# MLP of a hybrid decoder layer: first weight casts ahead of the first relus, the residual's scale and shift in four parts, other PSUM banks and another block order in the last group

## The chip, the cores and the metric

The kernel runs on one core of one Trainium2 chip. The metric is the device time of one execution in microseconds (us), as the median of several runs. PE is the matrix engine (TensorE), DVE the vector engine, ACT the scalar engine, POOL GpSimd, and SP the engine whose queue issues most transfers. Each engine runs its own instructions in the order in which the program emits them, and waits at an instruction until the semaphores of what it needs are set.

## The reference, cut to what matters

One decoder layer on 512 tokens and 16 meta tokens, width 1024, float32: attention and a recurrent mixer, then an output projection with a layer norm, then the MLP. The change touches the MLP alone:

```python
    h = layer_norm(ALPHA * h + merged @ w_out[l], ln1_g[l], ln1_b[l])
    ff = jnp.square(jax.nn.relu(h @ w_ff1[l])) @ w_ff2[l]      # 1024 -> 4096 -> 1024
    h = layer_norm(ALPHA * h + ff, ln2_g[l], ln2_b[l])
return h[:, N_META:]
```

## The kernel before, in words

Each float32 operand of a product is split into a rounded part (`hi`, by a cast on ACT) and its rest (`lo`, by a subtraction on DVE), and each product is the sum of three: hi by hi, lo by hi and hi by lo. So every weight tile costs a load on the SP queue, casts on ACT, subtractions on DVE, and then the matmuls.

**Up products.** The 4096 hidden columns are 32 tiles of 128. Tile f takes 24 matmuls of 128x512 (8 pieces of the width, three products each), then a relu on ACT (line 1604) and a square on DVE (line 1605), and lands in `ff`, a buffer for one group of 8 tiles, of which there are two. The first three tiles (`SPLITF`, lines 1530 to 1544) belong to the front part of the kernel, whose instructions stand in a fixed list (`ORDER`); they are computed in two halves of 256 tokens, in segments of six matmuls of 256 columns. The last segments in the list, by tile and segment of the second half, are (f0,1), (f0,2), (f1,2), (f1,3), (f2,2), (f0,3), (f2,3). Their weights lie in the three `whi` and three `wlo` slots of the pool `wst`, each slot cut into two halves of 512 columns: the first `whi` slot holds the second half of tile 1 and the first half of tile 2, the first `wlo` slot the first half of tile 1 and the second half of tile 2. A tile's first half is read by segments 0 and 1, its second by 2 and 3. The other tiles' weights go through the same slots in turn, beginning with the first.

**Down products.** The hidden columns are taken in four groups of 8 tiles (`NG`). In the first three groups the product of `ff` (two blocks of tokens t by two blocks of columns x) with w_ff2 (two blocks x by two halves of the output d) is made of seven block products in place of eight (`down`, lines 1670 to 1717), with sums and differences of blocks: the sums of weights are added on DVE (line 1685), the differences of hidden blocks too (line 1701), the right blocks are split by `split_right` (two tile pairs, from the rings `b` and `w`), the left block by `split_left` (ring `a`, two pairs). Each product is 24 matmuls into two PSUM banks, and is added into the residual `res` (four row blocks b, two halves d) by two DVE additions (line 1715). The pairs of banks are called u (up products), R, P and T. The last group (`last_group`, lines 1721 to 1765) makes the eight plain block products, and then ends each of the four row blocks: two additions (line 1745), statistics for each half (line 1566), their merging, a power on POOL, four scalings (lines 1572 and 1573) and two stores (`finish`).

**The residual.** Before the first down product is added, `res` is multiplied by ALPHA and ln1's gain (line 1771, eight instructions) and then gets ALPHA times ln1's offset added (eight more). `first_rows` loads both vectors, spread over all partitions, 512 KB each.

**The order.** All of this is a list of units: five up units (tiles 3 to 7), then up and down units in turn, then the last group. One loop (line 1799) emits them: at step i the loads of unit i+4, the preparation (casts, subtractions) of unit i+2, the matmuls of unit i, and its `post` (relu and square, additions, scalings). Before this loop, the relus and squares of the first three tiles are emitted. So ACT and DVE see three relus and squares, then the preparations of units 0 and 1, and so on; the eight scalings stand behind unit 2, the eight shifts behind unit 3, and the preparation of the first down unit (unit 6) comes behind those.

Of the kernel before, what the change touches and what calls it, by code (L numbers as in the profile page):

```python
# [20 lines left out]
P = 128  # L21
D = 1024
# [3 lines left out]
T = SEQ + NMETA  # L26
# [58 lines left out]
SPLITF = 3  # L85
# [296 lines left out]
def hybrid_layer_kernel(ctx: ExitStack, tc: tile.TileContext, I: dict, out: bass.AP):  # L382
# [1179 lines left out]
    st2 = [rp.tile([P, 2, 6], F32, name=f"gst{b}") for b in range(4)]  # L1562

    def finish(b, g2, b2):
        for n in range(2):
            dve.bn_stats(st2[b][:, n, :], res[b][n])  # L1566
# [64 lines left out]
    def block_of(g, t, x):  # L1631
        return ff[g].rearrange("p (i x) (t c) -> p i x t c", x=2, t=2)[:, :, x, t]
# [4 lines left out]
            nc.sync.dma_start(raws[g, x, d].rearrange("p i c -> p (i c)"), I["w_ff2"][(2 * g + x) * 2 + d])  # L1637
        return f

    def split_left(src):  # L1640
        hi, lo = pair_of("a")
        v = lambda t: t.rearrange("p (i c) -> p i c", c=256)
        act.copy(v(hi), src)
        dve.tensor_tensor(v(lo), src, v(hi).bitcast(F32), op=ALU.subtract)
        return hi, lo
# [11 lines left out]
    def products(left, right, acc, bs, first, last, again=False):  # L1657
        (ahi, alo) = left
        for b in bs:
            for i in range(NP):  # L1660
                bhi, blo = right[i // 2]
                as_ = slice(i * 256 + b * P, i * 256 + (b + 1) * P)
                ws = slice((i % 2) * 512, (i % 2 + 1) * 512)
                for q, (l, r) in enumerate(((ahi, bhi), (ahi, blo), (alo, bhi))):
                    pe.matmul(acc[b], l[:, as_], r[:, ws], start=first and i == 0 and q == 0,  # L1665
                              stop=last and i == NP - 1 and q == 2, skip_group_check=True)
# [3 lines left out]
    def down(g, n):  # L1670
        left, chain, updates = (
            ((1, 0),                 "R", (2, 0, ALU.add)),
            (((1, 1), (1, 0)), "T", (2, 0, ALU.add)),
            (((0, 1), (1, 0)), "R", (2, 1, ALU.subtract)),
            ((0, 1),                 "P", (0, 1, ALU.add)),
            (((1, 0), (0, 0)), "R", (0, 1, ALU.subtract)),
            (((1, 1), (0, 1)), "P", (2, 1, ALU.add)),
            (((0, 0), (0, 1)), "R", (0, 0, ALU.add)),
        )[n]
        first = n in (0, 1, 3)  # L1680
        loads = [[load_raw(g, 0, 0), load_raw(g, 1, 0)], [], [load_raw(g, 0, 1)], [load_raw(g, 1, 1)], [], [], [load_raw(g, 0, 0)]][n]
        s = {}

        def plus(a, b):
            dve.tensor_tensor(a, a, b, op=ALU.add)  # L1685
            return a

        def prep():
            x0, y0, x1, y1 = (raws.get((g, x, d)) for d in range(2) for x in range(2))
            if n == 0:  # L1690
                chains["sum"] = plus(x0, y0)
            elif n == 2:
                plus(chains["sum"], x1)
            elif n == 3:
                plus(chains["sum"], y1)
            elif n == 6:
                plus(x0, x1)
            right = (chains["sum"], y0, chains["sum"], chains["sum"], x1, y1, x0)[n]
            if isinstance(left[0], tuple):
                src = mp.tile([P, NP, 256], F32, name="dif", tag="dif", bufs=2)  # L1700
                dve.tensor_tensor(src, block_of(g, *left[0]), block_of(g, *left[1]), op=ALU.subtract)
            else:
                src = block_of(g, *left)
            s["r"] = split_right(right)
            s["l"] = split_left(src)

        def run():
            if first:
                chains[chain] = [psum(chain, i, f"dn{chain}") for i in range(2)]
            products(s["l"], s["r"], chains[chain], range(2), first, True)  # L1710

        def post():
            b, d, op = updates
            for i in range(2):
                dve.tensor_tensor(res[b + i][d], res[b + i][d], chains[chain][i], op=op)

        return Unit(loads, prep, run, post)
# [1 line left out]
    rows_ = {}  # L1719

    def last_group(g):
        accs, sets, lefts = {}, {}, {}

        def unit(t, x, ds, bs, loads=(), lefts_=(), rights=(), post=lambda: None):
            def prep():
                for x_, d in rights:
                    sets[x_, d] = split_right(raws[g, x_, d])
                for k in lefts_:
                    lefts[k] = split_left(block_of(g, *k))

            def run():
                for d in ds:
                    if (t, d) not in accs:
                        accs[t, d] = [psum(*[("R", i), ("T", i), ("P", i), ("u", i)][2 * t + d], "last") for i in range(2)]
                for b in bs:
                    for d in ds:
                        products(lefts[t, x], sets[x, d], accs[t, d], [b], x == 0, x == 1)

            return Unit(loads, prep, run, post)

        def done(t, b):
            def f():
                for d in range(2):
                    r = res[2 * t + b][d]
                    dve.tensor_tensor(r, r, accs[t, d][b], op=ALU.add)  # L1745
                finish(2 * t + b, rows_["g"], rows_["b"])
            return f

        def vectors():
            t = mp.tile([P, 2, D], F32, name="rows2", tag="ff", bufs=2)  # L1750
            rows_["g"], rows_["b"] = t[:, 0], t[:, 1]
            row_of(t[:, 0], "ln2_g")
            row_of(t[:, 1], "ln2_b")
# [12 lines left out]

    def scaled(name, k):
        def f():
            for b in range(4):
                for n in range(2):  # L1770
                    dve.scalar_tensor_tensor(  # L1771
                        res[b][n], *((res[b][n], ALPHA, rows_["1"][:, k, n * 512 : (n + 1) * 512]) if k == 0 else
                                     (rows_["1"][:, k, n * 512 : (n + 1) * 512], ALPHA, res[b][n])),
                        op0=ALU.mult, op1=(ALU.mult, ALU.add)[k])
        return f

    def first_rows():
        t = rows_["1"] = mp.tile([P, 2, D], F32, name="rows1", tag="braw", bufs=4)
# [1 line left out]
        row_of(t[:, 1], "ln1_b")  # L1780

    units = [up(f) for f in range(SPLITF, NF)]
    units[1].loads.append(first_rows)
    for i, k in ((2, 0), (3, 1)):
        was = units[i].post
        units[i].post = lambda was=was, k=k: (was(), scaled(None, k)())
    for g in range(NG - 1):
        f = (g + 1) * NF
        for n in range(7):
# [3 lines left out]
                units.append(up(f))  # L1793
                f += 1
            units.append(down(g, n))
    units += last_group(NG - 1)
    for f in range(SPLITF):
        up_evict(f, ups[f].t)
    for i in range(-LEAD[0], len(units)):
        if 0 <= i + LEAD[0] < len(units):  # L1800
            for f in units[i + LEAD[0]].loads:
                f()
        if 0 <= i + LEAD[1] < len(units):
            units[i + LEAD[1]].prep()
        if i >= 0:
            units[i].run()
            units[i].post()
# [52 lines left out]
```

## Time and profile before

| what | us |
|---|---|
| median of 3 runs | 918.55 (917.95 to 919.69) |
| the profiled execution, its own time | 918.13 |
| its span, first to last instruction | 916.4 |
| PE busy | 885.1 (97% of the span) |
| DVE, ACT, POOL busy | 668.6, 471.1, 245.8 |
| mean granted PE clock | 0.988 |

In the rows of a timeline the columns are: start (us from the span's start), us, engine, line of the kernel, operation, the tile written and the tiles read, the shape, how many; in brackets the idle time of the engine before and what ended it. Consecutive instructions of one kind are merged into one row. In the rows of the windows the busy time of PE, of its weight loads (PEld), of DVE, ACT and POOL follow one another, then the granted clock (1.00 is full speed), the share of the DMA engines and the GB/s. A line is that of a helper where the work goes through one: L466 to L468 are the three products of `three`, L1665 is the matmul of the down products.

### The profile page before, as it was taken

To read this page: it belongs to the slowest core of one execution; us is meant where nothing else is said; L and a number is where in the kernel's file an instruction comes from. 1 tells how busy PE (TensorE), PEld (TensorE's weight loads), DVE (VectorE), ACT (ScalarE), POOL (GpSimd) and SP (SyncE) were. 2 spreads that over 40 slices of the span, in tenths; PEclk is the share of its full clock that TensorE was granted. 3 is DMA by queue.
4 is the path that set the end of the run, shared out by engine and by line. 5 is a ranking of instruction groups with operands and counts; after the bars stand their busy time and mean duration, and the time that the engine had idled before them with its cause. 6 is when DMAs were issued, how large, how long until landed. Compare 5 with 4: busy or idle time off the path is not lost. (4 is left out here: it accounts for less than half of the span.)

```text
span 916.4 us, 16744 instructions
## 1 busy us (share of the span) xinstructions
PE 885.1 (97%) x6424; PEld 761.2 (83%) x6424; DVE 668.6 (73%) x1152; ACT 471.1 (51%) x1030; POOL 245.8 (27%) x652
## 2 busy tenths in 40 slices
PE   7999999999999999999999999989999999999895
PEld 6999989888998888978878778778888888888784
DVE  7873977869677697487586788488778777877647
ACT  7845568376583674565726548333433344443410
POOL 4137173381643804606538111000000000000001
PEclk9999999999999999999989999999999999999998
DMA  7453333424242242223245522432342343232302
GB/s 267 126 132 99 88 92 89 125 67 128 71 112 68 86 143 72 60 71 113 71 131 152 142 94 82 134 153 92 115 138 93 115 143 133 92 119 91 134 1 92
DMA packets 69496, 99.02 MB, mean 108 GB/s; under 512 B 39863, under 2 KB 47289, under 8 KB 66985
## 3 DMA queue, kind: packets, MB, share of 16 engines
q1 hardware_dynamic: 68576, 96.79, 34.2%
q8 instruction: 50, 0.82, 0.4%
q10 hardware_dynamic: 840, 1.17, 0.4%
q14 instruction: 30, 0.24, 0.1%
HBM read 90.78 MB, written 8.21 MB: 108 GB/s over the span
## 5 line engine op out<-in xcount | busy, mean ns | idle before, releaser
L466 PE MATMUL g<-hhi,whi 128*128 128x512 f32 (+3 forms) x640 | 212.9, 333 | 0.5 <-DVE GR L1057 0.5
L467 PE MATMUL g<-hlo,whi 128*128 128x512 f32 (+3 forms) x640 | 204.0, 319 | 1.7 <-DVE hlo L829 1.7
L468 PE MATMUL g<-hhi,wlo 128*128 128x512 f32 (+3 forms) x640 | 203.6, 318 | 0.1
L466 PEld LDWEIGHTS g<-hhi,whi 128*128 128x128 f32 x640 | 121.0, 189 | 12.9 <-issue 1.9
L467 PEld LDWEIGHTS g<-hlo,whi 128*128 128x128 f32 x640 | 121.1, 189 | 9.6 <-DVE hlo L829 2.1
L468 PEld LDWEIGHTS g<-hhi,wlo 128*128 128x128 f32 x640 | 121.0, 189 | 8.7 <-DVE wlo L625 0.4
L625 DVE TENSOR_TENSOR wlo<-wraw,whi 128x512 fp32r<-128x512 f32 x126 | 88.5, 709 | 30.4 <-ACT whi L623 29.7
L1134 POOL TENSOR_TENSOR ftmp<-Xf,Nf 108x84 f32<-108x84 f32 (+23 forms) x248 | 86.8, 350 | 75.4 <-DMA Nf<-Nd 45.2
L623 ACT CAST whi<-wraw 128x512 fp32r<-128x512 f32 x126 | 76.9, 618 | 55.6 <-PE g L467 23.9
L458 POOL TENSOR_TENSOR rsf<-rsf,mhalf 128x1 f32<-128x1 f32 x4 | 3.9, 987 | 341.9 <-DVE rsf L457 341.9
L1138 POOL TENSOR_TENSOR Xf<-Xf,ftmp 108x84 f32<-108x84 f32 (+23 forms) x248 | 90.0, 363 | 19.0
L466 PE MATMUL up<-h1hi,whi 128*128 128x512 f32 x232 | 91.0, 392 | 1.9 <-ACT whi L1618 1.9
L468 PE MATMUL up<-h1hi,wlo 128*128 128x512 f32 x232 | 90.9, 392 | 0.2 <-DVE wlo L1619 0.2
L467 PE MATMUL up<-h1lo,whi 128*128 128x512 f32 x232 | 90.8, 391 | 0.0
L1605 DVE TENSOR_TENSOR ff<-ff 128x512 f32<-128x512 f32 x32 | 21.9, 691 | 55.5 <-ACT ff L1604 55.5
L1604 ACT ACTIVATE ff<-up 128x512 f32<-128x512 f32 x29 | 17.3, 596 | 87.2 <-PE up L468 87.2
L1652 ACT CAST bhi<-braw 128x1024 fp32r<-128x1024 f32 x25 | 26.2, 1049 | 61.1 <-DVE braw L1685 53.1
L1240 ACT ACTIVATE Z<-g,PC 64x64 f32<-64x64 f32 x64 | 19.8, 310 | 65.2 <-DVE Z L1237 40.0
L466 PEld LDWEIGHTS up<-h1hi,whi 128*128 128x128 f32 x232 | 43.8, 189 | 11.0 <-ACT whi L1618 2.1
L468 PEld LDWEIGHTS up<-h1hi,wlo 128*128 128x128 f32 x232 | 43.8, 189 | 10.1 <-DVE wlo L1619 0.9
L467 PEld LDWEIGHTS up<-h1lo,whi 128*128 128x128 f32 x232 | 43.9, 189 | 9.1
L1618 ACT CAST whi<-wraw 128x1024 fp32r<-128x1024 f32 x29 | 30.3, 1048 | 23.2 <-PE dnR L1665 12.0
(406 smaller groups left out, 2044.3 us busy)
## 6 DMA issues: line engine op xcount, KB each, us to landing
wraw<-in_w_in_dram SPq DMA_DIRECT2D x52, 512.0 KB
braw<-in_w_ff_dram SPq DMA_DIRECT2D x19, 1024.0 KB
wraw<-in_w_ff_dram SPq DMA_DIRECT2D x32, 512.0 KB
wraw<-in_w_out_dram SPq DMA_DIRECT2D x14, 256.0 KB
Nf<-Nd SPq DMA_DIRECT2D x24, 144.0 KB
res<-in_x_dram SPq DMA_DIRECT2D x4, 512.0 KB
G<-in_consts_dram SPq DMA_DIRECT2D x16, 128.0 KB
XB<-xtd SPq DMA_DIRECT2D x16, 128.0 KB
```

Source lines behind the costliest of these rows:

```text
L466: pe.matmul(ps, whi, xhi, start=first, stop=False)
L467: pe.matmul(ps, whi, xlo, start=False, stop=False)
L468: pe.matmul(ps, wlo, xhi, start=False, stop=last)
L623: AC(512, lambda hi=hi, qs=qs: act.copy(hi.t, raw.t[:, qs]), plain=True, r=[raw], w=[hi], new=[hi])
L625: f = lambda hi=hi, lo=lo, qs=qs, e=e: e.tensor_tensor(lo.t, raw.t[:, qs], hi.t.bitcast(F32), op=ALU.subtract)
L1134: sub(nj * nt, lambda s=s, nj=nj, nt=nt, tv=tv: pool.tensor_tensor(tv(), Xf.t[:, 0:nj, s : s + 1].to_broadcast([NB, nj, nt]), Nf.t[:, s : ...
L1138: sub(nj * nt, lambda s=s, nj=nj, tv=tv: pool.tensor_tensor(Xf.t[:, 0:nj, s + 1 :], Xf.t[:, 0:nj, s + 1 :], tv(), op=ALU.add), port=1, r=[ ...
L1240: op("ACT", 335, lambda: act.activation(Z.t[H2[1], c, 1, :], src(1), AF.Copy, scale=PC.t[H2[1], last : last + 1]), r=[ps, PC], w=[(Z, ("s" ...
L1604: act.activation(t, ps, AF.Relu)
L1605: dve.tensor_tensor(t, t, t, op=ALU.mult)
L1618: act.copy(hi, s["raw"])
L1652: act.copy(hi, src)
```

## The change

- `finish` no longer takes the statistics of the two halves. `done` takes each half's statistics right behind the addition that ends this half.
- `split_left` may be told which tiles to write. In the last group the left block (0,1) goes into two tiles of the ring `dif`, the block (1,1) into one tile of the ring `ff`, and the others into the ring `a` as before.
- In the seven-product groups, the second product (n = 1, banks T) is no longer added into `res` after each group. It stays in its PSUM banks over the groups, and the last group goes on adding its own block (t = 1, d = 0) to it.
- The last group runs over d = 0 first: four units with one block product each, (t,x) = (0,0), (1,0), (0,1), (1,1); then d = 1: four units, one for each row block, with both of its block products. The banks are P for (t = 0, d = 0), T for (1,0), u for (0,1) and R for (1,1). The additions and statistics of d = 0 come behind the third and the fourth unit, those of d = 1 and `finish` behind the last four. Each of the first four units loads one weight block, and ln2's vectors go into a slot of the weight blocks' ring `braw`, not of `ff`.
- The scale and shift of the residual is cut in four parts, one for each pair of row blocks t and half n: two scales, then two shifts. They come behind units 1, 2, 3 and 4, in the order (t,n) = (1,0), (1,1), (0,1), (0,0). The loads of ln1's vectors move from unit 1's loads to unit 3's.
- The relus and squares of the first three tiles are emitted inside the loop: that of tile 0 behind the preparation of unit 0, those of tiles 1 and 2 behind the preparation of unit 1.

```diff
     def finish(b, g2, b2):
-        for n in range(2):
-            dve.bn_stats(st2[b][:, n, :], res[b][n])
         mv = rp.tile([P, 2], F32, name=f"gmv{b}")
...
-    def split_left(src):
-        hi, lo = pair_of("a")
+    def split_left(src, room=None):
+        hi, lo = room or pair_of("a")
...
-        first = n in (0, 1, 3)
+        first = n in (0, 3)
...
         def run():
-            if first:
+            if first or chain not in chains:
                 chains[chain] = [psum(chain, i, f"dn{chain}") for i in range(2)]
-            products(s["l"], s["r"], chains[chain], range(2), first, True)
+            products(s["l"], s["r"], chains[chain], range(2), first or n == 1 and g == 0, n != 1)
 
         def post():
+            if n == 1:
+                return
...
     def last_group(g):
-        accs, sets, lefts = {}, {}, {}
-
-        def unit(t, x, ds, bs, loads=(), lefts_=(), rights=(), post=lambda: None):
+        sets, lefts = {}, {}
+        accs = {(1, 0): chains["T"]}
+
+        def room(t, x):
+            if (t, x) == (0, 1):
+                return tuple(mp.tile([P, D], F32R, name="a" + q, tag="dif", bufs=2) for q in ("hi", "lo"))
+            if (t, x) == (1, 1):
+                t = mp.tile([P, 2, D], F32R, name="aw", tag="ff", bufs=2)
+                return t[:, 0], t[:, 1]
+            return pair_of("a")
+
+        def unit(parts, loads=(), lefts_=(), rights=(), post=lambda: None):
...
             def run():
-                for d in ds:
+                for t, x, d, bs in parts:
                     if (t, d) not in accs:
-                        accs[t, d] = [psum(*[("R", i), ("T", i), ("P", i), ("u", i)][2 * t + d], "last") for i in range(2)]
+                        accs[t, d] = [psum({(0, 0): "P", (0, 1): "u", (1, 1): "R"}[t, d], i, "last") for i in range(2)]
+                    products(lefts[t, x], sets[x, d], accs[t, d], bs, x == 0 and (t, d) != (1, 0), x == 1)
+
+            return Unit(loads, prep, run, post)
+
+        def done(t, d, bs):
+            def f():
                 for b in bs:
-                    for d in ds:
-                        products(lefts[t, x], sets[x, d], accs[t, d], [b], x == 0, x == 1)
...
-                finish(2 * t + b, rows_["g"], rows_["b"])
+                    dve.bn_stats(st2[2 * t + b][:, d, :], r)
+                    if d == 1:
+                        finish(2 * t + b, rows_["g"], rows_["b"])
             return f
...
-            unit(0, 0, (0,), both, [load_raw(g, 0, 0), load_raw(g, 0, 1)], [(0, 0)], [(0, 0)]),
-            unit(1, 0, (0,), both, [load_raw(g, 1, 0), load_raw(g, 1, 1)], [(1, 0)]),
-            unit(1, 0, (1,), both, [vectors], (), [(0, 1)]),
-            unit(0, 0, (1,), both, (), (), [(1, 1)]),
-            unit(0, 1, both, (0,), (), [(0, 1)], [(1, 0)], done(0, 0)),
-            unit(0, 1, both, (1,), (), [], (), done(0, 1)),
-            unit(1, 1, both, (0,), (), [(1, 1)], (), done(1, 0)),
-            unit(1, 1, both, (1,), (), (), (), done(1, 1)),
+            unit([(0, 0, 0, both)], [load_raw(g, 0, 0)], [(0, 0)], [(0, 0)]),
+            unit([(1, 0, 0, both)], [load_raw(g, 1, 0)], [(1, 0)]),
+            unit([(0, 1, 0, both)], [load_raw(g, 0, 1)], [(0, 1)], [(1, 0)], done(0, 0, both)),
+            unit([(1, 1, 0, both)], [load_raw(g, 1, 1)], [(1, 1)], [(0, 1)], done(1, 0, both)),
+        ] + [
+            unit([(t, 0, 1, (b,)), (t, 1, 1, (b,))], [vectors] if t + b == 0 else (), (), [(1, 1)] if t + b == 0 else (), done(t, 1, (b,)))
+            for t in range(2) for b in range(2)
         ]
...
+    def scaled(t, n):
+        for k in range(2):
+            v = rows_["1"][:, k, n * 512 : (n + 1) * 512]
+            for b in (2 * t, 2 * t + 1):
+                r = res[b][n]
+                if k == 0:
+                    dve.scalar_tensor_tensor(r, r, ALPHA, v, op0=ALU.mult, op1=ALU.mult)
+                else:
+                    dve.scalar_tensor_tensor(r, v, ALPHA, r, op0=ALU.mult, op1=ALU.add)
...
-    units[1].loads.append(first_rows)
-    for i, k in ((2, 0), (3, 1)):
+    units[3].loads.append(first_rows)
+    for i, at in ((1, (1, 0)), (2, (1, 1)), (3, (0, 1)), (4, (0, 0))):
...
-    units += last_group(NG - 1)
-    for f in range(SPLITF):
-        up_evict(f, ups[f].t)
-    for i in range(-LEAD[0], len(units)):
...
         if 0 <= i + LEAD[1] < len(units):
             units[i + LEAD[1]].prep()
+        if i < 0 and i + LEAD[1] >= 0:
+            for f in ((0,), (1, 2))[i + LEAD[1]]:
+                up_evict(f, ups[f].t)
         if i >= 0:
             units[i].run()
             units[i].post()
```

More of the change, by code (lines that the diff above doesn't have):

```diff
@@ L1728, in prep @@
                 for k in lefts_:
-                    lefts[k] = split_left(block_of(g, *k))
+                    lefts[k] = split_left(block_of(g, *k), room(*k))
             def run():
-                for d in ds:
+                for t, x, d, bs in parts:
                     if (t, d) not in accs:
-                        accs[t, d] = [psum(*[("R", i), ("T", i), ("P", i), ("u", i)][2 * t + d], "last") for i in range(2)]
-                for b in bs:
-                    for d in ds:
-                        products(lefts[t, x], sets[x, d], accs[t, d], [b], x == 0, x == 1)
@@ L1739, in unit @@
[L1739 to L1743, printed above, removed]
+                        accs[t, d] = [psum({(0, 0): "P", (0, 1): "u", (1, 1): "R"}[t, d], i, "last") for i in range(2)]
[3 more added lines that the diff above has]
+            def f():
+                for b in bs:
                     r = res[2 * t + b][d]
@@ L1745, in f @@
                     dve.tensor_tensor(r, r, accs[t, d][b], op=ALU.add)
-                finish(2 * t + b, rows_["g"], rows_["b"])
+                    dve.bn_stats(st2[2 * t + b][:, d, :], r)
+                    if d == 1:
+                        finish(2 * t + b, rows_["g"], rows_["b"])
             return f
         def vectors():
-            t = mp.tile([P, 2, D], F32, name="rows2", tag="ff", bufs=2)
-            rows_["g"], rows_["b"] = t[:, 0], t[:, 1]
-            row_of(t[:, 0], "ln2_g")
@@ L1753, in vectors @@
-            row_of(t[:, 1], "ln2_b")
+            v = mp.tile([P, 2, D], F32, name="rows2", tag="braw", bufs=4)
+            rows_["g"], rows_["b"] = v[:, 0], v[:, 1]
+            row_of(v[:, 0], "ln2_g")
+            row_of(v[:, 1], "ln2_b")
         both = (0, 1)
         return [
-            unit(0, 0, (0,), both, [load_raw(g, 0, 0), load_raw(g, 0, 1)], [(0, 0)], [(0, 0)]),
-            unit(1, 0, (0,), both, [load_raw(g, 1, 0), load_raw(g, 1, 1)], [(1, 0)]),
-            unit(1, 0, (1,), both, [vectors], (), [(0, 1)]),
@@ L1760, in last_group @@
-            unit(0, 0, (1,), both, (), (), [(1, 1)]),
-            unit(0, 1, both, (0,), (), [(0, 1)], [(1, 0)], done(0, 0)),
-            unit(0, 1, both, (1,), (), [], (), done(0, 1)),
-            unit(1, 1, both, (0,), (), [(1, 1)], (), done(1, 0)),
-            unit(1, 1, both, (1,), (), (), (), done(1, 1)),
-        ]
[L1767 to L1775, printed above, removed]
+            unit([(0, 0, 0, both)], [load_raw(g, 0, 0)], [(0, 0)], [(0, 0)]),
@@ L1782, in hybrid_layer_kernel @@
     units = [up(f) for f in range(SPLITF, NF)]
-    units[1].loads.append(first_rows)
-    for i, k in ((2, 0), (3, 1)):
+    units[3].loads.append(first_rows)
+    for i, at in ((1, (1, 0)), (2, (1, 1)), (3, (0, 1)), (4, (0, 0))):
         was = units[i].post
-        units[i].post = lambda was=was, k=k: (was(), scaled(None, k)())
+        units[i].post = lambda was=was, at=at: (was(), scaled(*at))
     for g in range(NG - 1):
@@ L1795, in hybrid_layer_kernel @@
             units.append(down(g, n))
-    units += last_group(NG - 1)
-    for f in range(SPLITF):
-        up_evict(f, ups[f].t)
-    for i in range(-LEAD[0], len(units)):
+    ends = []
+    for i in range(-LEAD[0], NMAIN := len(units) + 8):
+        if i + LEAD[0] == len(units) and not ends:
+            ends = last_group(NG - 1)
+            units += ends
         if 0 <= i + LEAD[0] < len(units):
```

## The prediction

> **What bounds the kernel now.** I read the page first: TensorE (PE) is busy nearly throughout, so time is to be had only where it stands still or runs slowly, and behind its last matmul. Then came the waits of PE from 568 us on, where the changed code begins, the busy time by windows, and the timelines of PE, VectorE (DVE), ScalarE (ACT) and the SP queue around each wait. The span, and what PE waited for:
>
> ```profile
> span 916.4 us, 16744 instructions
> ```
>
> ```profile
> PE last L1665 <- ACT whi L1652: 2.9, 1, 2.9
> PE up L466 <- ACT whi L1618: 1.9, 1, 1.9
> PE dnR L1665 <- ACT ahi L1643: 1.6, 1, 1.6
> ```
>
> Busy time by window (PE, PEld, DVE, ACT, POOL, then granted clock, DMA share, GB/s), one steady stretch and three short ones, and one unit's 24 matmuls from the chain that ended last:
>
> ```profile
> 574.00:576.00 2.00, 2.00 (x19) 2.00 (x18) 0.00 (x0) 0.00 (x0) 0.00 (x0) 1.00 0.00 0
> ...
> 626.00:700.00 74.00, 74.00 (x328) 61.27 (x327) 54.84 (x54) 28.61 (x32) 0.00 (x0) 1.00 0.34 121
> ```
>
> ```profile
> 581.00:582.00 1.00, 0.79 (x3) 0.68 (x3) 1.00 (x2) 0.00 (x0) 0.00 (x0) 0.50 0.00 0
> ...
> 862.00:863.00 1.00, 1.00 (x6) 0.82 (x5) 1.00 (x2) 1.00 (x2) 0.00 (x0) 1.00 0.00 0
> ```
>
> ```profile
> 630.26 5.44 PE dnT L1665 x24
> ```
>
> Between the waits PE never pauses (74.00 of 74 us), and every up or down unit takes 5.44 us, 0.227 per matmul. DVE has 54.84 of 74 there, so DVE work removed from the steady part (six T evictions) is worth nothing: PE hides it. What can be won lies in four places.
>
> ```profile
> 577.81 0.28 PE L468 MATMUL g<-h1hi,wlo 128*128 128x256 f32 x1
> 579.97 0.62 PE L466 MATMUL up<-h1hi,whi 128*128 128x512 f32 x1 [1.88 <-ACT whi L1618]
> ...
> 581.23 0.80 PE L468 MATMUL up<-h1hi,wlo 128*128 128x512 f32 x1 [0.21 <-DVE wlo L1619]
> ...
> 587.44 0.39 PE L466 MATMUL up<-h1hi,whi 128*128 128x512 f32 x1
> ```
>
> ```profile
> 614.41 0.39 PE L468 MATMUL up<-h1hi,wlo 128*128 128x512 f32 x1
> 616.44 0.50 PE L1665 MATMUL dnR<-bhi,ahi 128*128 128x512 f32 x1 [1.64 <-ACT ahi L1643]
> ...
> 618.09 0.79 PE L1665 MATMUL dnR<-bhi,alo 128*128 128x512 f32 x1 [0.91 <-DVE alo L1644]
> ...
> 624.65 0.39 PE L466 MATMUL up<-h1hi,whi 128*128 128x512 f32 x1
> ```
>
> ```profile
> 858.35 0.39 PE L1665 MATMUL dnR<-whi,alo 128*128 128x512 f32 x1
> 861.59 0.47 PE L1665 MATMUL last<-bhi,ahi 128*128 128x512 f32 x1 [2.86 <-ACT whi L1652]
> ```
>
> ```profile
> 904.99 0.39 PE L1665 MATMUL last<-whi,alo 128*128 128x512 f32 x1
> ```
>
> The loop's first up unit could begin at 577.81+0.12 = 577.93; its second begins at 587.44, 9.5 us later for 5.44 us of work. The first down product ends at 624.65, 10.0 us after 614.64. The last group starts 3.0 us late (861.59 against 858.58), and 11.2 us follow PE's end at 905.22. From 624.65 to 858.58 run 43 units without a gap: 233.93/5.44.
>
> **First casts ahead of the first relus.** The order on ACT and DVE now:
>
> ```profile
> 577.41 1.57 ACT L1604 ACTIVATE ff<-g 128x512 f32<-128x512 f32 x3 [4.74 <-PE g L468]
> 578.86 2.00 ACT L1618 CAST whi<-wraw 128x1024 fp32r<-128x1024 f32 x2
> ```
>
> ```profile
> 579.95 2.36 DVE L1619 TENSOR_TENSOR wlo<-wraw,whi 128x1024 fp32r<-128x1024 f32 x2
> ```
>
> The cast waits behind three relus, which wait for PE, and PE then waits for the cast and its rest (wlo). The data is there: DMA is quiet from 574 us. With the cast in front, what holds it is its slot, still read by the split up products. The plan's order ends with the segments (f1,2), (f1,3), (f2,2), (f0,3), (f2,3) of six matmuls, 0.72 us each. The first whi slot holds f1's second half and f2's first; its last reader ends three segments before the end, at 575.8, so the cast is done by 576.9. The first wlo slot holds f2's second half, which the very last segment reads. So wlo starts 0.20 us after 577.93 (that is what a relu takes to follow PE: 598.52 below against 587.44+2x5.44 = 598.32), and its reader 1.28 later (581.23-579.95), at 579.41. PE runs two matmuls at 577.93, pauses 1.0, and ends the unit at 579.41+22x0.227 = 584.40 in place of 587.44: **3.04 us**. Nothing then waits for the relus soon: their results are first read for the down product. From below: if the whi slot too came free only at the end, 0.7 to 1.95 (first rival); from above, without any wait for wlo, 577.93+5.44 = 583.37, 4.07. A slow clock behind the 1.0 us pause would cost up to the 1.2 worked out there; I take full clock, since the pause is half of the one that brought it, and 3.04, which goes by the slots.
>
> **Scale and shift in four parts.** Before, the eight scales stand behind the third unit and the eight shifts behind the fourth; the sum of two weight blocks for the first down product waits for them all, then ACT casts it and DVE makes the rests:
>
> ```profile
> 598.52 0.60 ACT L1604 ACTIVATE ff<-up 128x512 f32<-128x512 f32 x1 [3.90 <-PE up L468]
> ...
> 613.45 1.05 ACT L1652 CAST bhi<-braw 128x1024 fp32r<-128x1024 f32 x1 [8.89 <-DVE braw L1685]
> ```
>
> ```profile
> 599.15 0.69 DVE L1605 TENSOR_TENSOR ff<-ff 128x512 f32<-128x512 f32 x1 [3.27 <-ACT ff L1604]
> 599.76 4.90 DVE L1771 SCALAR_TENSOR_TENSOR res<-res,rows 128x512 f32<-128x512 f32 x8
> ...
> 606.31 4.91 DVE L1771 SCALAR_TENSOR_TENSOR res<-rows,res 128x512 f32<-128x512 f32 x8
> 611.12 2.29 DVE L1685 TENSOR_TENSOR braw<-braw 128x2048 f32<-128x2048 f32 x1
> 614.54 1.23 DVE L1653 TENSOR_TENSOR blo<-braw,bhi 128x1024 fp32r<-128x1024 f32 x1 [1.12 <-ACT bhi L1652]
> ...
> 616.81 1.22 DVE L1644 TENSOR_TENSOR alo<-ff,ahi 128x1024 fp32r<-128x1024 f32 x1
> ```
>
> After, only the third part, four instructions, stands between the fourth unit's square and that sum; the fourth part comes behind the product's preparation. Let E be the fourth unit's end. The part begins at E+1.44 (599.76-598.32) and takes 4x0.60 = 2.41; the sum to the first cast 2.33, that cast to blo 1.09, blo to alo 2.27, alo to its reader 1.28: alo is ready at E+10.82. PE comes to its reader at E+2x5.44+0.45 = E+11.33. So the stall goes, with 0.5 us to spare. With E = 584.40+3x5.44 = 600.72 the down product runs from 611.60 to 617.04, where it was 624.65: 7.61 in all, and less the 3.04 above **4.57 us**, the two pauses and the slow clock behind them. If the spare 0.5 is missed, the delay comes back one for one, at most the 4.57. What follows is DVE's fourth part, 2.41 in a stretch where PE has ten us of work for it.
>
> The vectors for this (ln1_g, ln1_b) are now asked for two units later on SP, behind two weight loads that wait for slots:
>
> ```profile
> 567.60 0.86 SPq L1560 DMA_DIRECT2D rows<-in_rows_dram  x2
> ```
>
> ```profile
> 581.20 9.58 SPq L1614 DMA_DIRECT2D wraw<-in_w_ff_dram  x4
> ```
>
> The third unit's load went out at 581.20, when the first wlo was done; now that is 579.4, and the fourth's and the vectors' behind the second wlo about 581.9. Before they took under 6.4 us (567.60 to the quiet 574), so 588.3; first needed at 584.40+5.44+1.44 = 591.3. Three us hide it.
>
> **Banks and order in the last group.** Before, the first product writes the R banks, which the down product just before it filled, and DVE's evictions stand behind a split whose cast waits for that product's slot:
>
> ```profile
> 858.55 1.04 ACT L1643 CAST ahi<-ff 128x1024 fp32r<-128x1024 f32 x1 [4.61 <-PE dnR L1665]
> ```
>
> ```profile
> 853.99 1.22 DVE L1644 TENSOR_TENSOR alo<-ff,ahi 128x1024 fp32r<-128x1024 f32 x1
> ...
> 860.77 1.28 DVE L1715 TENSOR_TENSOR res<-res,dnR 128x512 f32<-128x512 f32 x2
> ```
>
> The first eviction ends about 861.4 and PE starts at 861.59: the bank decided, though the view of waits names ACT. After, that product writes P, evicted one unit earlier, with operands that were ready at 855.3 (the last is alo, from 853.99): **3.1 us** (the wait and 0.1 of a slower first matmul). Next late is the second unit's left block, which still waits for the down product; cast and rest take 2.3, under the 5.44 of cover. The T sum stays in its banks, which costs no wait: nothing else writes them. The loads of the group's weight blocks move from two per unit to one, and ln2's vectors into a slot of theirs, on the same SP queue; each is still asked for four units (21.8 us) ahead of its unit's products, the vectors five ahead of their use, against the 6.4 us above for a megabyte, so I cost them at nothing; the slots that the third and fourth left blocks now take (dif, ff) were last read by earlier groups' splits.
>
> **The tail.** DVE's work per finished row block now, the last of four:
>
> ```profile
> 900.76 1.28 DVE L1745 TENSOR_TENSOR res<-res,last 128x512 f32<-128x512 f32 x2
> ...
> 906.89 1.28 DVE L1745 TENSOR_TENSOR res<-res,last 128x512 f32<-128x512 f32 x2
> 908.09 1.28 DVE L1566 BATCH_NORM_STATS2 gst<-res 128x6 f32<-128x512 f32 x2
> ```
>
> One block takes DVE 6.13 us (906.89-900.76) against PE's 5.44, so it falls behind: the last add starts at 906.89, not at 905.22+0.20. After, the d=0 add and its statistics are done units earlier under PE; 6.13-1.2 = 4.93 is left, under 5.44, and the lag of **1.47 us** goes. Of the last block itself one add (0.60, from 906.89 to 908.09 for two) and one statistics (0.60) leave the path: **1.2 us**. If DVE still lagged, 1.2 alone; more than 2.7 has no source.
>
> **Sum.** 3.04+4.57+3.1+1.47+1.2 = 13.4 us. The profiled execution took 918.13 with its span of 916.4; it becomes 904.7 with a span of 903.0. The median of before is 0.42 above the profiled run, so I put the median after at 905.2.
>
> **Rivals.** *The first cast gets its slot only when all split products are done* (the change then does not do what it says). Cast at 578.13, first matmul 1.11 later (579.97-578.86), third at 578.13+1.09+1.28 = 580.50, the unit ends at 585.49: 1.95 gained in place of 3.04, so 906.3. PE would then stand idle 2.1 us in two pieces (1.31 and 0.81), as much as at 578 to 581, where the granted clock fell to 0.50 and cost 1.2 more (581.23+22x0.227 = 586.22 against 587.44): 907.5. For it: no row shows the slots apart, since the cast always came late. Against: the segment order. The clock need not fall: behind the 2.86 us at 858.6 it stayed 1.00. [...]
>
> *The first down product is still late.* DVE's chain has 0.5 to spare; two us of delay give 907.2, the whole old stall 909.8. For it: six DVE and three ACT steps in a row; against, each is from this trace.
>
> *The last group waits all the same*, for a cast in place of a bank: 3.1 back, 908.3. For it: ACT and the slots are tight around 858; against, all operands of its first product stood there at 855.3.
>
> *DVE hangs on the vectors.* The first part waits in DVE's order for ln1's rows, and behind it stand the rests of the fifth and sixth units' weights, two squares and two parts: 2x2.41+2.36+2x0.6 = 8.4 before the third part, which must begin by 602.7. Rows landing after 594.3 cost one us each: even at 607.7, slower behind that; at 612 the time is 922.9. Against: that is 30 us after the issue where 6.4 were enough.
>
> **Chances.** Forecast 0.72; late slot 0.12; late down product 0.07; late last group 0.04; vectors 0.05, of which 0.03 slower and 0.02 within 0.2% (1.8 us, about what a measurement here can tell). Range 903.4 to 907.9: below, the first gain at its upper end and the 0.6 by which the runs of before lie under their median; above, the late slot with the slow clock and that spread. Faster 0.95, same 0.02, slower 0.03.
>
> **What would show it.** Right: PE's first wait ends on wlo near 579.4, no wait before the first down product, its end near 617, no pause and no R eviction before `last`, the last add 0.2 us behind PE, span near 903. Wrong: a pause of over a us at any of these, granted clock 0.50 after 577 us, SP or DVE waiting for rows.

## The result, and the profile after

The changed kernel takes 904.13 us (median of 4 runs, 903.63 to 905.25) against 918.62 for the kernel before (4 runs): a ratio of 0.9843, 95% interval 0.9826 to 0.986. The profiled execution took 903.63 us with a span of 901.8, so the span is 14.6 us shorter than before; forecast were 13.4 (range 903.4 to 907.9 us for the median). In the list of what PE waited for, nothing is left behind 572 us; the whole list from 560 us on is one wait that was there before too:

```profile
PE g L1511 <- DVE res L1505: 0.2, 1, 0.2
```

The windows show PE busy in every us from the last split products to the end of the first down product and through the last group, at full granted clock; only the tail is left (columns as before the prediction):

```profile
577.70:615.80 38.10, 38.10 (x170) 31.55 (x169) 29.01 (x36) 15.13 (x20) 0.00 (x0) 1.00 0.56 195
```

```profile
849.50:893.30 43.80, 43.80 (x194) 36.05 (x192) 30.92 (x43) 8.86 (x9) 2.96 (x3) 1.00 0.09 32
893.30:901.80 8.50, 0.10 (x1) 0.00 (x0) 4.57 (x8) 0.00 (x0) 0.99 (x1) 0.74 0.24 93
```

PE's timeline at the four places, each the counterpart of rows in the prediction:

```profile
577.58 0.28 PE L468 MATMUL g<-h1hi,wlo 128*128 128x256 f32 x1
577.70 0.40 PE L466 MATMUL up<-h1hi,whi 128*128 128x512 f32 x1
...
583.16 0.39 PE L466 MATMUL up<-h1hi,whi 128*128 128x512 f32 x1
...
610.14 0.39 PE L468 MATMUL up<-h1hi,wlo 128*128 128x512 f32 x1
610.36 0.39 PE L1663 MATMUL dnR<-bhi,ahi 128*128 128x512 f32 x1
...
615.80 0.39 PE L466 MATMUL up<-h1hi,whi 128*128 128x512 f32 x1
...
849.50 0.39 PE L1663 MATMUL dnR<-whi,alo 128*128 128x512 f32 x1
849.72 0.39 PE L1663 MATMUL last<-bhi,ahi 128*128 128x512 f32 x1
...
893.02 0.39 PE L1663 MATMUL last<-whi,aw 128*128 128x512 f32 x1
```

The loop's first unit follows the split products at once and takes 5.46 us; the first down product follows the up product at once; so does the last group. What made this possible on ACT and DVE, and the tail on DVE:

```profile
573.46 1.05 ACT L1616 CAST whi<-wraw 128x1024 fp32r<-128x1024 f32 x1 [1.05 <-PE g L467]
577.17 0.60 ACT L1602 ACTIVATE ff<-g 128x512 f32<-128x512 f32 x1 [2.67 <-PE g L468]
```

```profile
575.79 1.22 DVE L1617 TENSOR_TENSOR wlo<-wraw,whi 128x1024 fp32r<-128x1024 f32 x1 [2.66 <-PE g L468]
...
600.92 1.28 DVE L1781 SCALAR_TENSOR_TENSOR res<-res,rows 128x512 f32<-128x512 f32 x2
602.13 1.29 DVE L1783 SCALAR_TENSOR_TENSOR res<-rows,res 128x512 f32<-128x512 f32 x2
603.33 2.28 DVE L1683 TENSOR_TENSOR braw<-braw 128x2048 f32<-128x2048 f32 x1
...
609.01 1.22 DVE L1642 TENSOR_TENSOR alo<-ff,ahi 128x1024 fp32r<-128x1024 f32 x1
...
851.92 1.28 DVE L1715 TENSOR_TENSOR res<-res,dnR 128x512 f32<-128x512 f32 x2
...
893.44 0.69 DVE L1752 TENSOR_TENSOR res<-res,last 128x512 f32<-128x512 f32 x1 [0.29 <-PE last L1663]
894.16 0.69 DVE L1753 BATCH_NORM_STATS2 gst<-res 128x6 f32<-128x512 f32 x1
```

The cast now stands 3.7 us ahead of the first relu. Four scalings stand between a square and the sum of weight blocks, where sixteen instructions stood in two lots. The R banks are evicted at 851.92, after the last group has begun at 849.72. The last addition starts 0.19 us behind PE's end at 893.25.

### The profile page after: what moved, and what is told of

It is laid out like the page before. It is cut to its first block, busy times and chain, and to the rows that moved or that the text cites. A ratio compares the mean times of both kernels' runs of the same rounds, so it can differ in the third digit from the quotient of the medians.

```text
span 901.8 us, 16735 instructions
## 1 busy us (share of the span) xinstructions
PE 881.0 (98%) x6424; PEld 759.8 (84%) x6424; DVE 666.6 (74%) x1146; ACT 470.9 (52%) x1030; POOL 245.5 (27%) x652
```

## The experiments

The front part of the kernel, up to the last split up product, which no edit touches, ended between 576.7 and 578.4 us in the profiles. To compare stages, times are therefore counted from S, the end of the last split product in each profile. "Down" is the end of the first down product, "rest" the time from there to the end of the span; both come from PE's rows in the manner of the last section (before: 624.65-577.93 and 916.4-624.65). Each ratio given below is against runs of the kernel before on the same chip.

| kernel | median us | S | S to down | rest |
|---|---|---|---|---|
| before | 918.6 | 577.93 | 46.72 | 291.75 |
| after | 904.13 | 577.70 | 38.10 | 286.00 |
| 1 casts first alone | 913.86 | 577.50 | 42.84 | 291.66 |
| 2 four parts alone | 915.82 | 577.25 | 42.17 | 293.08 |
| 3 banks alone | 914.27 | 576.69 | 47.24 | 288.57 |
| 4 order and T alone | 916.57 | 578.40 | 47.38 | 289.12 |
| 5 first slot | 905.11 | 577.83 | 39.30 | 286.07 |
| 6 second slot | 905.66 | 577.22 | 40.20 | 286.08 |
| 7 T undone | 903.87 | 578.12 | 38.10 | 286.08 |
| 8 two parts | 906.64 | 577.78 | 40.11 | 286.01 |
| 9 finish's order | 903.21 | 577.90 | 38.11 | 285.39 |

### 1. The casts ahead of the relus, alone (on the kernel before)

```diff
-    for f in range(SPLITF):
-        up_evict(f, ups[f].t)
     for i in range(-LEAD[0], len(units)):
...
             units[i + LEAD[1]].prep()
+        if i < 0 and i + LEAD[1] >= 0:
+            for f in ((0,), (1, 2))[i + LEAD[1]]:
+                up_evict(f, ups[f].t)
```

> The kernel before with one part alone: the first casts ahead of the first relus. Theory (the four gains add): PE goes from the split up products to the loop's first unit without a pause, so the second unit begins 5.44 us after them (9.51 before), and everything behind moves by the same 4.1 us: the first down product still waits for the scalings, which hang on the end of the fourth unit; about 914.5 us. Rival (the sixteen scalings on DVE decide when the first down product starts, whenever the units before it end): the 4.1 us are lost again there, 918.6.

Measured: 913.86 us, ratio 0.9941 (0.9923 to 0.9958). PE's waits behind 572 us, in full: the first pause is gone, the other two have the same lengths as before.

```profile
PE last L1665 <- ACT whi L1652: 2.9, 1, 2.9
PE dnR L1665 <- ACT ahi L1643: 1.6, 1, 1.6
PE dnR L1665 <- DVE alo L1644: 0.9, 1, 0.9
```

From S to the end of the first down product it is 3.88 us less than before, and the rest is unchanged. The rival, by which DVE's scalings would swallow the gain, is out: their place in time hangs on PE's fourth unit. Of the 4.07 that the first pause cost, 0.19 is missing. The half clock behind the second pause accounts for most of it. In the kernel before, by the windows in the last section, it began at 617.74, some 0.35 us before the second wait ended at 618.09; the first matmul behind that wait took 0.79 us, and the next five 0.63 each. Here the first, at 613.61, took 0.65 us, so that part of it still ran at full clock, and the next seven 0.63 each: all of the slow stretch fell on matmuls.

### 2. Scale and shift in four parts, alone (on the kernel before)

```diff
-    units[1].loads.append(first_rows)
-    for i, k in ((2, 0), (3, 1)):
+    units[3].loads.append(first_rows)
+    for i, at in ((1, (1, 0)), (2, (1, 1)), (3, (0, 1)), (4, (0, 0))):
```

with the new `scaled` of the change.

> The kernel before with one part alone: scale and shift in four parts, with the later load of their vectors. Theory: the first pause of PE stays, with its slow clock; the pause before the first down product goes, with the slow clock behind it: 4.5 us, about 914.1. Rival (DVE and ACT have too many steps for the first down product even so, or the vectors come late): half the pause stays, 916.4 or more.

Measured: 915.82 us, ratio 0.9962 (0.9947 to 0.9978), 1.7 us more than the theory had. The profiled execution is the fastest of the ten, at 914.32. In it the stage itself did what was said: 4.55 us less from S to the end of the down product. But the rest is 1.33 us longer, and that lies in the last group, which this edit does not touch. The granted clock behind the same wait of 2.86 us, here and in the kernel before:

```profile
856.40:857.40 1.00, 1.00 (x3) 0.81 (x4) 1.00 (x2) 1.00 (x2) 0.00 (x0) 0.50 0.00 0
857.40:858.40 1.00, 1.00 (x4) 0.81 (x3) 1.00 (x2) 0.74 (x1) 0.00 (x0) 0.50 0.00 0
858.40:859.40 1.00, 1.00 (x4) 0.79 (x3) 1.00 (x2) 0.00 (x0) 0.00 (x0) 0.50 0.00 0
859.40:860.40 1.00, 1.00 (x6) 0.77 (x5) 1.00 (x2) 0.00 (x0) 0.00 (x0) 0.99 0.00 0
```

```profile
861.60:862.60 1.00, 1.00 (x5) 0.82 (x6) 1.00 (x2) 1.00 (x2) 0.00 (x0) 1.00 0.00 0
862.60:863.60 1.00, 1.00 (x6) 0.84 (x5) 1.00 (x2) 0.79 (x1) 0.00 (x0) 1.00 0.00 0
```

In experiment 2 over three us at half clock follow; before, none. So in the profiled execution what is missing of the forecast gain is the clock behind a pause that this kernel still has, not the parts. That this holds for the median too is argued, not shown: all ten executions had a mean granted clock of 0.986 to 0.988, no higher than the 0.988 of the profiled kernel before, though one of its slow stretches had gone.

### 3. The first product's banks, alone (on the kernel before)

```diff
-                        accs[t, d] = [psum(*[("R", i), ("T", i), ("P", i), ("u", i)][2 * t + d], "last") for i in range(2)]
+                        accs[t, d] = [psum(*[("P", i), ("T", i), ("R", i), ("u", i)][2 * t + d], "last") for i in range(2)]
```

> The kernel before with only the banks of its last group's sums changed: (t=0,d=0) in P, (0,1) in T, (1,0) in R, (1,1) in u; order and all else as before. Theory (the wait in front of the last group is the wait for the eviction of the R banks): the wait of 2.9 us goes, with 0.1 of a slower first matmul, 915.5. Rival (the wait is for the cast that the view of waits names): it stays, 918.6.

Measured: 914.27 us, ratio 0.9945 (0.9923 to 0.9966). PE goes into the last group without a gap, while DVE evicts the R banks later:

```profile
857.62 0.39 PE L1665 MATMUL dnR<-whi,alo 128*128 128x512 f32 x1
857.85 0.39 PE L1665 MATMUL last<-bhi,ahi 128*128 128x512 f32 x1
```

```profile
860.05 1.28 DVE L1715 TENSOR_TENSOR res<-res,dnR 128x512 f32<-128x512 f32 x2
```

The rest is 3.18 us shorter than before. The median is 1.2 us under the forecast 915.5; in the profile S came 1.24 us earlier than before, in code that the edit does not touch. Casts and their order were not touched, so the view of waits named the wrong engine: the wait was for the bank.

### 4. The last group's order, with T kept, alone (R banks first)

The last group and the T sums of the change on a kernel that is otherwise the one before. Against the changed kernel's last group, the banks of the first and the last pair are exchanged:

```diff
-                        accs[t, d] = [psum({(0, 0): "P", (0, 1): "u", (1, 1): "R"}[t, d], i, "last") for i in range(2)]
+                        accs[t, d] = [psum({(0, 0): "R", (0, 1): "u", (1, 1): "P"}[t, d], i, "last") for i in range(2)]
```

> The kernel before with only the last group's new order (d = 0 first, its additions and statistics early, T kept in its banks over the groups), but with its first product in the R banks as before and the relus and scalings as before. Theory: the two pauses and the 3 us in front of the last group stay; DVE keeps up with PE, the last addition starts 0.2 us behind PE, and 8.3 us in place of 9.5 follow it: 2.6 us, 916.0. Rival (DVE lags all the same): only 1.2 us, 917.4.

Measured: 916.57 us, ratio 0.9967 (0.9952 to 0.9982). The last addition follows PE's last matmul (906.11+0.23 = 906.34) by 0.20 us:

```profile
906.54 0.69 DVE L1752 TENSOR_TENSOR res<-res,last 128x512 f32<-128x512 f32 x1 [0.29 <-PE last L1663]
```

The rest is 2.63 us shorter, as forecast. From S to down it takes 0.66 us longer than before, though the edit does not touch this stretch. Both slow stretches of the clock began later against the waits, so that less of them fell into these: the two matmuls behind the first wait took 0.50 and 0.40 us, where before they took 0.62 and 0.63, and the first behind the last wait 0.62, where before it took 0.79; and behind the waits for wlo and alo six and seven matmuls took 0.63 us each, where before four and five did.

Stage by stage, the four parts alone give 3.88+4.55+3.18+2.63 = 14.24 us; all together give 8.62+5.75 = 14.37. They add.

### 5. The first slot for the first weights (on the changed kernel)

```diff
-            hi, lo = s["w"] = pair_of("w")
+            hi, lo = s["w"] = (whole_hi[0], whole_lo[0]) if f == SPLITF else pair_of("w")
```

where `whole_hi` and `whole_lo` are the pool's `whi` and `wlo` tiles from the setup.

> The changed kernel, with the loop's first unit made to take the first whi and the first wlo slot, the ones the prediction had in mind, where it takes the third of each now. Theory (what delayed PE in the prediction and not on the chip is which slot the first weights get): the cast starts near 575.6, wlo only 0.2 us behind the last split product, PE runs two matmuls, pauses 1.0 us and ends the first unit 1.0 us later than in the changed kernel, without a slow clock: 905.2 us. Rival (the slots do not matter, the release works otherwise than read): no pause, 904.1.

Measured: 905.11 us, ratio to before 0.9844 (0.9829 to 0.9858).

```profile
577.83 0.40 PE L466 MATMUL up<-h1hi,whi 128*128 128x512 f32 x1
578.07 0.40 PE L467 MATMUL up<-h1lo,whi 128*128 128x512 f32 x1
579.37 0.50 PE L468 MATMUL up<-h1hi,wlo 128*128 128x512 f32 x1 [0.91 <-DVE wlo L1619]
```

This is the picture that the prediction had: two matmuls, then the wait for wlo, whose reader starts 1.54 us behind S (forecast 1.48). From S to down it is 1.20 us more than in the changed kernel, which is the 1.0 of the theory plus a slower first matmul behind the wait (0.50 against 0.39). The times alone do not settle it: the medians are 1.0 apart, but the ratios, each to its own runs of the kernel before, are 0.9844 here and 0.9843 for the changed kernel.

### 6. The second slot for the first weights (on the changed kernel)

The same edit with `whole_hi[1], whole_lo[1]`.

> The changed kernel, with the loop's first unit made to take the second whi and the second wlo slot; the whi slot is read by the very last split product. Theory: the cast starts 0.2 us behind the last split product, PE stands still 1.3 and then 0.8 us, and the first unit ends 2.0 us later than in the changed kernel: 906.2; if the granted clock falls to half, as behind the pause of before, 1.2 us more, 907.4. Rival (slots do not matter): no pause, 904.1.

Measured: 905.66 us, ratio to before 0.9854 (0.9837 to 0.9872).

```profile
577.10 0.28 PE L468 MATMUL g<-h1hi,wlo 128*128 128x256 f32 x1
578.39 0.50 PE L466 MATMUL up<-h1hi,whi 128*128 128x512 f32 x1 [1.02 <-ACT whi L1618]
578.73 0.40 PE L467 MATMUL up<-h1lo,whi 128*128 128x512 f32 x1
579.65 0.50 PE L468 MATMUL up<-h1hi,wlo 128*128 128x512 f32 x1 [0.53 <-DVE wlo L1619]
579.99 0.39 PE L466 MATMUL up<-h1hi,whi 128*128 128x512 f32 x1
```

That is the first rival's case: 2.10 us more from S to down than in the changed kernel, for 2.0 expected. The window behind the second wait has full granted clock:

```profile
579.40:580.40 1.00, 0.75 (x3) 0.66 (x4) 1.00 (x3) 1.00 (x3) 0.00 (x0) 1.00 0.00 0
580.40:581.40 1.00, 1.00 (x6) 0.78 (x6) 1.00 (x2) 0.36 (x1) 0.00 (x0) 1.00 0.44 131
```

So slots decide, and even the worst of the three, at full clock, would have kept half of the first gain.

### 7. T added after each group again (on the changed kernel)

```diff
-        first = n in (0, 3)
+        first = n in (0, 1, 3)
...
-            if n == 1:
-                return
...
-        accs = {(1, 0): chains["T"]}
+        accs = {}
```

and `(1, 0): "T"` among the last group's new banks.

> The changed kernel without one part: the second product of each of the first three groups is again added into the residual after each group, and the last group starts its sum for (t=1,d=0) anew. Theory (PE hides DVE's work in the steady part): no change, 904.1, with 3.6 us more of busy DVE. Rival (the six additions delay a preparation that PE waits for): up to 3.6 us slower, 907.7.

Measured: 903.87 us, ratio to before 0.9829 (0.9813 to 0.9845). From S to down 38.10 and the rest 286.08, against 38.10 and 286.00. The additions put back, 3.6 us of DVE by the estimate above, made PE wait nowhere: its list of waits behind 572 us is empty, as in the changed kernel. Keeping T in its banks is worth nothing, as the prediction said.

### 8. Two parts ahead of the first down product's sum (on the changed kernel)

```diff
-    for i, at in ((1, (1, 0)), (2, (1, 1)), (3, (0, 1)), (4, (0, 0))):
+    for i, at in ((1, (1, 0)), (2, (1, 1)), (3, (0, 1)), (3, (0, 0))):
```

> The changed kernel with the fourth part of scale and shift moved ahead, behind the fourth unit and so before the sum for the first down product, which then stands behind eight instructions in place of four. Theory (the chain from the fourth unit's end to the down product's third matmul has 0.5 us to spare, and beyond that each us costs one): 2.4 us more in the chain, so PE reads alo 1.9 us late, 906.0; with the slow clock behind such pauses up to 907.2. Rival (there is more to spare than counted): under 0.5 us, 904.5 or less.

Measured: 906.64 us, ratio to before 0.9863 (0.9848 to 0.9878).

```profile
610.22 0.39 PE L468 MATMUL up<-h1hi,wlo 128*128 128x512 f32 x1
611.14 0.50 PE L1663 MATMUL dnR<-bhi,ahi 128*128 128x512 f32 x1 [0.53 <-ACT ahi L1641]
611.48 0.40 PE L1663 MATMUL dnR<-blo,ahi 128*128 128x512 f32 x1
612.77 0.50 PE L1663 MATMUL dnR<-bhi,alo 128*128 128x512 f32 x1 [0.90 <-DVE alo L1642]
```

S to down is 2.01 us more than in the changed kernel: 2.4 more in the chain less the spare 0.5 gives the 1.9 of the theory. The clock stayed full here too, in the profiled execution, which is the fastest of the four; the others took 906.17 to 908.02 us, and no trace shows their clock by stage:

```profile
612.80:613.80 1.00, 1.00 (x4) 0.83 (x5) 1.00 (x2) 1.00 (x2) 0.00 (x0) 1.00 0.02 8
```

### 9. The order of the closing scalings (on the changed kernel)

```diff
+        qs = [slice(q * 512, (q + 1) * 512) for q in range(2)]
         for q in range(2):
-            qs = slice(q * 512, (q + 1) * 512)
-            dve.scalar_tensor_tensor(res[b][q], res[b][q], mv[:, 0:1], g2[:, qs], op0=ALU.subtract, op1=ALU.mult)
-            dve.scalar_tensor_tensor(res[b][q], res[b][q], r, b2[:, qs], op0=ALU.mult, op1=ALU.add)
-            (nc.sync, nc.scalar)[q].dma_start(out[0, b * P : (b + 1) * P, qs], res[b][q])
+            dve.scalar_tensor_tensor(res[b][q], res[b][q], mv[:, 0:1], g2[:, qs[q]], op0=ALU.subtract, op1=ALU.mult)
+        for q in range(2):
+            dve.scalar_tensor_tensor(res[b][q], res[b][q], r, b2[:, qs[q]], op0=ALU.mult, op1=ALU.add)
+            (nc.sync, nc.scalar)[q].dma_start(out[0, b * P : (b + 1) * P, qs[q]], res[b][q])
```

> The changed kernel, with the four scalings at the end of a row block in another order: both that need only the mean first, then both that need the power from POOL, where now the two kinds alternate. Theory (behind PE's last matmul all is one chain, in which DVE stands still 0.44 us for the power): the second half's first scaling fills that wait, and the end comes 0.4 to 0.5 us earlier, 7.9 us in place of 8.4 behind the last addition; 903.7, less than the runs' spread, so to be read from the trace. Rival (the chain is bound by the stores): no difference in the tail.

Measured: 903.21 us, ratio to before 0.9845 (0.9825 to 0.9864), not told apart from the changed kernel by the times. The trace shows the step: both scalings by the mean run on without a break, the power is there when they end, and the span ends 7.75 us behind the last addition (901.4-893.65) where the changed kernel needs 8.36 (901.8-893.44): 0.61 less, for 0.4 to 0.5 expected.

```profile
893.65 0.69 DVE L1753 TENSOR_TENSOR res<-res,last 128x512 f32<-128x512 f32 x1 [0.94 <-PE last L1664]
...
895.41 1.40 DVE L1570 SCALAR_TENSOR_TENSOR res<-res,gmv,rows 128x512 f32<-128x512 f32 x2
896.73 1.41 DVE L1572 SCALAR_TENSOR_TENSOR res<-res,rsf,rows 128x512 f32<-128x512 f32 x2
```

## Why the prediction was right, and the one term that was off

**First casts: right in its mechanism, the size too small by 1.0 us.** The term was 3.04; PE's pause was gone entirely, and the measured gain is 9.51-5.44 = 4.07, the upper bound. The wait for wlo near 579.4, which was named as a sign of being right, did not come. The step that failed is the premise behind "The first whi slot holds f1's second half and f2's first": the slot does hold these, but the loop's first weights do not go to the first slots, and the text ahead of the prediction was wrong to say that the other tiles begin there. In the changed kernel they lie in the third `whi` and the third `wlo` slot. By the kernel's fixed list of slots (`SLOTS`), the third slots hold the first halves of tiles 0 and 1 (whi), and tile 0's first and tile 1's second half (wlo), and the rows above fit these alone: the cast starts at 573.46, 0.2 us behind the last reader of whi in segment (f0,1), and wlo at 575.79, 0.2 us behind the end of (f1,3), three segments before 577.70. Experiment 5 puts the weights where the prediction had them and brings its pause back.

**Four parts: right.** 4.57 forecast; 4.55 measured alone, and 8.62-4.07 = 4.55 in the whole. The spare 0.5 us is there: alo is ready at 609.01+1.22+0.06 = 610.29, its reader runs at 610.82. That beyond it one us costs one was tried in experiment 8: 2.01 us for 1.9. The vectors' loads went out at 580.4, and DVE's first part began at 590.0 with no wait for them:

```profile
580.37 1.20 SPq L1560 DMA_DIRECT2D rows<-in_rows_dram  x2
```

```profile
590.04 1.29 DVE L1781 SCALAR_TENSOR_TENSOR res<-res,rows 128x512 f32<-128x512 f32 x2
```

The rival of the vectors, the one that ended slower, did not arise; how late they could be was not tried.

**Banks: right.** 3.1 forecast, 3.18 measured alone, and no gap in the whole. That the bank decided, against what the view of waits named, was argued from one eviction's end and is shown by experiment 3.

**Tail: right.** 2.67 forecast; the lag of the last addition fell from 1.67 to 0.19 us, and what follows it from 9.51 to 8.36: 1.48+1.15 = 2.63, the same in experiment 4 alone.

**The sum.** Measured from S, 14.37 us; the forecast's 13.38 and the 1.03 of the first term make 14.41. The profiled execution's span gained another 0.23 in the untouched front part (S at 577.70 against 577.93). The range was written a little low: by its own terms its ends are 905.2-1.03-0.6 = 903.6 and 907.5+0.6 = 908.1.

**The clock as a rival's price.** The prediction priced the late slot with and without the slow clock behind its pauses; in the profiled execution of experiment 6 it stayed full (1.00 in each window from 578.40 to 583.40), so that rival would have given the smaller loss there. Its four executions took 904.63 to 907.77 us, and whether the slow clock came in the longest is not shown.

## What to carry to other kernels

Where one engine is busy 97% of the time, look at the few places where it stands still and follow each back to the instruction that stands in front of the late one in another engine's queue: here moving a cast ahead of three relus, spreading sixteen scalings in front of one sum, and changing one pair of banks were worth 11.8 of 14.4 us, and work taken off a busy but hidden engine nothing. When a buffer's slot decides a wait, find out which slot the program really takes, since the price here went from 0 to 2.1 us with the slot alone. Pauses removed one by one added up here (14.24 us alone, 14.37 together), where each hung on the same engine's progress, but a pause that stayed was charged differently by the clock (the 2.86 us: 1.00 behind it before, 0.50 in experiment 2), so compare stages and not only totals.

## What was not expected of the hardware

The same pause can cost the clock or not. PE's wait of 2.86 us in front of the last group was followed by full clock in the kernel before (1.00 in the windows from 861.60 on) and by 3.4 us at 0.50 in experiment 2, where the rest was 1.33 us longer, with the same instructions around it. In the kernel before, shorter waits (1.88 and 0.21 us; 1.64 and 0.91) each came with 3.4 us at 0.50, while the pauses of experiments 6 and 8 (1.02 and 0.53; 0.53 and 0.90) were followed by none in the profiled executions (1.00 in each window from 578.40 to 583.40 and from 612.80 to 617.00).

Nor did the slow stretches begin where a wait ended. Four windows of the kernel before, with the clock between full and half:

```profile
579.90:581.00 1.10, 1.03 (x2) 0.32 (x2) 1.09 (x2) 0.97 (x2) 0.00 (x0) 0.63 0.00 0
...
583.00:584.00 1.00, 1.00 (x4) 0.76 (x4) 0.00 (x0) 0.00 (x0) 0.00 (x0) 0.70 0.86 336
...
617.00:618.00 1.00, 0.18 (x1) 0.00 (x0) 1.00 (x2) 1.00 (x2) 0.00 (x0) 0.87 0.00 0
...
621.00:622.00 1.00, 1.00 (x6) 0.80 (x5) 1.00 (x2) 0.46 (x1) 0.00 (x0) 0.92 0.58 168
```

If the clock is 1.00 in one part of such a window and 0.50 in the other, a window of one us with 0.87 had 0.50 for 0.26 us of it, and both ends of each stretch can be worked out: 580.2 to 583.6 and 617.74 to 621.16 in the kernel before, and 856.0 to 859.4 in experiment 2 (from 0.95 over 853.40 to 856.30 and 0.99 over 859.40 to 860.40), about 3.4 us each. The first began 0.2 us behind the end of the wait of 1.88 us (579.97), the two others some 0.35 us before the ends of the waits of 0.91 and 2.86 us (618.09 and 856.36).

So the length of a wait alone did not tell what it cost. What decides it is not shown; no run was made to tell.

The kernel before spread from 916.2 to 921.9 us over 23 runs (mean granted clock 0.992 in the fastest and 0.985 in the slowest), where the changed kernel, which has no such pause, lay within 1.6 us in 4 (0.992 to 0.994). That the clock behind the pauses makes part of this spread is argued, not shown.
